# Reordering products and casts in the front stage of a hybrid attention and convolution layer

## The chip, the cores and the metric

The kernel runs on one core of a Trainium2 chip. A core has TensorE (PE, matrix products into PSUM), VectorE (DVE), ScalarE (ACT), GpSimd (POOL) and SyncE (SP), which here issues transfers; each works through its own list of instructions in order, and they meet at semaphores. The metric is the device time of one execution in microseconds, taken as the median of several runs. A profile is one further execution with its own time. PEld is the loading of weights into PE, which overlaps PE's products. "Slab", "chunk" and "half" are words of the kernel, explained below.

## The reference

The layer takes 1024 latent tokens `x` and 256 context tokens `ctx`, each of 1024 numbers, in float32. Cut to what matters:

```python
shift, scale, gate = split(silu(c) @ w_ada + b_ada)          # and the same for c_ctx
h  = rmsnorm(x,   norm_g) * (1 + scale)   + shift
hc = rmsnorm(ctx, norm_g) * (1 + scale_c) + shift_c
q, k, v, za, u, bg, cg, zc = split(h @ w_in)                 # eight groups of 512 columns
kc, vc = split(hc @ w_in[:, 512:1536])
attn = neighbourhood_attention(rms(q), rms(k), v, rms(kc), vc, rpb) * silu(za)
conv = bg * conv3(cg * u) * silu(zc)
out  = x + gate * (concat(attn, conv) @ w_out)
```

The change concerns the first two lines of work: `shift` and `scale` out of `w_ada`, and `h` itself, with the first columns of `h @ w_in`.

## The kernel before

**Numbers in two parts.** Products that need full accuracy are made of three products of rounded parts: a value is split into a high part (a cast, on ACT) and a low part (value minus high part, on DVE), and PE computes high by high, high by low and low by high. So every weight that comes from memory costs a cast on ACT and a subtraction on DVE before PE can use it, and `h` exists as `hh` and `hl`. All instructions issued through the wrapper `ordered` carry line 55 in the profile, so they are told apart by their tiles.

**The front stage** (lines 546 to 880). `w_ada`'s columns for shift and scale come in eight *slabs* of 1024 rows by 256 columns: slab (m, j) gives columns for two of the eight column blocks k = 2m and 2m + 1 of `h`, with j = 0 for shift and 1 for scale. For m = 0 and 1, `products(m, j)` (line 605) multiplies the slab as it is, in plain float32, eight products (16 records in the profile); for m = 2 and 3 `split(m, j, part)` (line 596) first casts the slab in two parts into `slabh` (ACT) and `slabl` (DVE), and `products` then runs 8 products on `slabh` and 8 on `slabl`. The third slabs are those with m = 2, the second ones m = 1. `row_copy(m)` (ACT for m > 0) and `modulation(m)` (four small transposes and a few DVE steps into `ab`) turn the result into per-row shift and scale.

`transposed(half, k)` (line 661) brings column block k of four of x's eight row tiles into PSUM with four PE transposes, and `turn(half, k, on)` (line 667) makes `hh[k]` and `hl[k]` of that half: one ACT activation (`h<-tr`), a second activation or a DVE step (`hw<-tr`, on ACT or DVE by its argument `on`), and a DVE subtraction (`h<-hw,h`). `first_columns(half, k)` (line 686) then runs nine matmuls of 128 by 512 with *chunk* k of `w_in`: three with the high weights (needing `hh`), three with the low weights, three with `hl`.

The tiles of `tr` (line 521) have two buffers. Products of a slab pair hold one from `products(m, 0)` until `modulation(m)` has read it; meanwhile the blocks of transposes share the other, so the next block waits until the `turn` of the one before has read it.

The two functions between which the change moves work on PE (lines 605 to 614 and 661 to 665), shortened:

```python
def products(m, j, kts=range(KT)):
    if m not in mods:
        mods[m] = tr()
    rows = mods[m][:2 if m < 2 else 4, 256 * j:256 * j + 256]
    parts = [(c2, slabs[m, j])] if m < 2 else [(c4, highs[j]), (c4, lows[j])]
    for i, (c, part) in enumerate(parts):
        for kt in kts:
            pe.matmul(rows, c[:, kt], part[:, kt], ...)

def transposed(half, k, ts=range(4)):
    if (half, k) not in pts:
        pts[half, k] = tr()
    for i in ts:
        pe.transpose(pts[half, k][:, i * P:(i + 1) * P], xx[4 * half + i][:, k * P:(k + 1) * P], ident)
```

**Order and transfers.** In this stage the order of the four engines and of SP is the program's order (`strict`, line 524): an instruction waits for the one ahead of it on its engine, however early its own data are there. SP issues all transfers here. Slabs after the first pair share three buffers with `xc` (the context tokens, line 791), with the tables `rw8` (`gains_load`, line 697) and with `rg` (`gains`, line 706): slab (2, 1) goes where (1, 0) was, (3, 0) where (1, 1) was, (3, 1) where (2, 0) was, `xc` where (2, 1) was, the tables where (3, 0) was, `rg` where (3, 1) was. `gains` is four POOL steps that write `rg`; SP stores it to memory (`rope_d<-rg`) and then loads the weights of the projection, `chunk_load(CQ, k)` for k = 0 to 7, into the five buffers `wr`, each of which is free once the cast and the subtraction of an earlier chunk are done (`chunk_split`, line 166: `wh<-wr` on ACT, `wl<-wr,wh` on DVE). Behind these on SP stand `bias_tables` (line 720, 8 and 16 small transfers named `t_d`), and behind them the loads of the next stage.

**After the front stage** the projection runs in 32 tiles `pacc` with products of the convolution's and gates' columns (`pu`) between them, then attention by quarters of heads (scores, exponentials, `po`), and the output projection `pout`. Tiles of the projection are normalised and rotated on ACT and DVE and turned by PE (`trA`, `trB`, line 226). The first unit of gate columns is loaded as `uraw` at the start of that stage (line 1175) and cast on ACT (`uh`).

Of the kernel before, what the change touches and what calls it, by code (L numbers as in the profile page):

```python
# [23 lines left out]
KT = D // P  # L24
# [12 lines left out]
CQ, CK, CV, CZA, CU, CBG, CCG, CZC = (512 * i for i in range(8))  # L37


def body(tc, es, x, ctxt, w_ada, b_ada, w_in, q_g, k_g, rpbr, w_out, vecs, cst, out):  # L40
# [100 lines left out]
    def place(k, shape, dtype, name):  # L141

        return hpool.tile(shape, dtype, name=name, tag=f"h{k}")
# [16 lines left out]
    def chunk_load(col, k):  # L160
        raw = wpp.tile([P, 3, P], F32, name="wr", tag="wr", bufs=5)
        chunk_anchor[:] = [sp.dma_start(raw, bass.AP(w_in.tensor, w_in.offset + (k * P) * 4096 + col,
                                                     [[4096, P], [512, 3], [1, P]]))]
        return raw
# [356 lines left out]
    def tr():  # L521
        return ps0.tile([P, 512], F32, name="tr", tag="tr", bufs=2)
# [9 lines left out]
    def load_slab(m, j):  # L532

        new = place(6 + j, [P, KT, 256], F32, "slab") if m == 0 else sl.tile([P, KT, 256], F32, name="slab", tag="slab", bufs=3)
        n = 2 if m == 0 else 1
        for i in range(n):
            rows = slice(KT // n * i, KT // n * (i + 1))
            sp.dma_start(new[:, rows], bass.AP(w_ada.tensor, w_ada.offset + j * D + 256 * m + 3 * D * P * rows.start,
                                               [[3 * D, P], [3 * D * P, KT // n], [1, 256]]))
        slabs[m, j] = new  # L540

    def load_chunks(ks):
        for k in ks:
            chunks[k] = chunk_load(CU, k)
# [51 lines left out]
    def split(m, j, part):  # L596

        if part == 0:
            highs[j] = hcp.tile([P, KT, 256], F32R, name="slabh", tag="AB"[j])
            lows[j] = place(6 + j, [P, KT, 256], F32R, "slabl")  # L600
        rows = slice(4 * part, 4 * part + 4)
        act.copy(highs[j][:, rows], slabs[m, j][:, rows])
        dve.tensor_tensor(lows[j][:, rows], slabs[m, j][:, rows], highs[j][:, rows].bitcast(F32), ALU.subtract)
# [9 lines that stand above are left out]
                pe.matmul(rows, c[:, kt], part[:, kt], start=(i == 0 and kt == 0 and j == 0),  # L613
                          stop=(i == len(parts) - 1 and kt == KT - 1 and j == 1), skip_group_check=True)
# [25 lines left out]
    def modulated(hi, lo, ps, k, w, on, between=None):  # L640

        n = len(ps.shape) > 2 and 512 or 256
        sh, sc = (ab[:, k, 2 * w + j:2 * w + j + 1] for j in range(2))
        hw = bmp.tile([P, 512], F32, name="hw", tag="kc_s", bufs=2)
        hv = hw[:, :n]
        if n == 512:
            hv = hv.rearrange("p (r b c) -> p r b c", r=8, b=8)
        act.activation(hi, ps, AF.Identity, bias=sh, scale=sc)
        if on is act:
            act.activation(hv, ps, AF.Identity, bias=sh, scale=sc)  # L650
        else:
            dve.tensor_scalar(hv, ps, sc, sh, ALU.mult, ALU.add)
        if between:
            between()
        dve.tensor_tensor(lo, hv, hi.bitcast(F32), ALU.subtract)

    def rows_of(v, half):

        return v.rearrange("p (b r c) -> p r b c", b=8, r=16)[:, 8 * half:8 * half + 8]
# [7 lines that stand above are left out]
    def turn(half, k, on, between=None):  # L667

        modulated(rows_of(hh[k], half), rows_of(hl[k], half),
                  pts.pop((half, k))[:].rearrange("p (r b c) -> p r b c", r=8, b=8), k, 0, on, between)  # L670
# [26 lines left out]
    def gains_load():  # L697

        rw = sl.tile([P, 2048], F32, name="rw8", tag="slab", bufs=3)
        gqk = rw[:, 1024:1152].rearrange("p (n d) -> p n d", n=2)  # L700
        for n, g in enumerate((q_g, k_g)):
            sp.dma_start(gqk[:, n], g.broadcast_to([P, HD]))
        sp.dma_start(rw[:, 0:1024], cst[:, P + 2:P + 1026])
        return rw, gqk

    def gains(tables):

        rw, gqk = tables
        pool.tensor_scalar(gqk[:, 0], gqk[:, 0], 0.125, None, ALU.mult)
        gkc1 = cp.tile([P, 1, HD], F32, name="gkc")  # L710
        pool.tensor_tensor(gkc1[:, 0], gqk[:, 0], gqk[:, 1], ALU.mult)
        rg = sl.tile([P, 2, NB, 2, HD], F32, name="rg", tag="slab", bufs=3)
        for n in range(2):
            rraw = rw[:, 512 * n:512 * n + 512].rearrange("p (b d) -> p b d", d=HD)
            for k in range(2):
                pool.tensor_tensor(rg[:, n, :, k], rraw, gqk[:, k:k + 1].broadcast_to([P, NB, HD]), ALU.mult)
        sp.dma_start(rope_d, rg[:].rearrange("p n b k d -> p (n b k d)"))
        return gkc1[:]
# [52 lines left out]
    turn(1, 0, act)  # L771
    load_slab(2, 1)
    load_chunks([4, 5])
    transposed(1, 1)
    products(1, 1)
    load_slab(3, 0)
    split_chunk(2)
    turn(1, 1, act)
# [7 lines left out]
    modulation(1, rw)  # L786
    turn(0, 2, dve)
    split(2, 0, 1)
    split(2, 1, 0)
    split(2, 1, 1)  # L790
    xc = sl.tile([P, 2, D], F32, name="xc", tag="slab", bufs=3)
    sp.dma_start(xc, ctxt[0].rearrange("(i p) d -> p i d", p=P))
    first_columns(1, 1)
# [2 lines left out]
    for m in range(1, 4):  # L796
        k, new, last = 2 * m, m < 3, m == 3
        turn(1, k, act)
        if m == 2:
            gkc = gains(tables)  # L800
            ch = [chunk_load(CQ, k) for k in range(4)]
        first_columns(0, k)
        transposed(0, k + 1)
        if new:
            products(m + 1, 0)
        turn(0, k + 1, dve)
        if m == 1:
            split(3, 0, 0)
            split(3, 0, 1)
            tables = gains_load()  # L810
        if m == 2:
            for i in range(2):
                square(xc[:, i], i)
            root(0)
            root(1)
            norm(xc[:, 0], 0)
            norm(xc[:, 1], 1)
        if last:
            transposed_ctx(0)
            ch[4] = chunk_split(ch[4])  # L820
            turn_ctx(0)
            bias_tables()
        first_columns(1, k)
        if new:
            split_chunk(k + 2)
            products(m + 1, 1)
            rw = row_copy(m + 1)
        transposed(1, k + 1)
        first_columns(0, k + 1, (0,))
        if last:  # L830
            transposed_ctx(1)
        if new:
            modulation(m + 1, rw)
        turn(1, k + 1, act)
        if new:
            split_chunk(k + 3)
        if m == 1:
            split(3, 1, 0)
        if m == 2:
            ch[0:2] = map(chunk_split, ch[0:2])  # L840
            ch += [chunk_load(CQ, k) for k in (4, 5)]
        if last:
            turn_ctx(1)
        first_columns(0, k + 1, (1, 2))
        if new:
            transposed(0, k + 2)
            if m == 2:
                more_h(range(6, KT))
            turn(0, k + 2, dve)
        if m == 1:  # L850
            split(3, 1, 1)
        if m == 2:
            ch[2:4] = map(chunk_split, ch[2:4])
            ch += [chunk_load(CQ, k) for k in (6, 7)]
        if last:
            group0 = conv_group(0, {u: acc0[n] for n, u in enumerate((CU, CBG, CCG))})
            next(group0)
            do_acts()
            do_dves()
            transposed_ctx(2)  # L860
            ch[5] = chunk_split(ch[5])
            turn_ctx(2)
            first_columns(1, k + 1, (0,))
            transposed_ctx(3)
            ch[6] = chunk_split(ch[6])
            first_columns(1, k + 1, (1,))
            ch[7] = chunk_split(ch[7])
            turn_ctx(3)
            first_columns(1, k + 1, (2,))
        else:  # L870
            first_columns(1, k + 1)
            transposed(1, k + 2)
# [294 lines left out]
    for n in range(NT + 3):  # L1167
# [21 lines left out]
        if t == 0 and 0 < n < NT:  # L1189
            nxt += map(chunk_split, raws)  # L1190
            ch, nxt, raws = nxt, [], []
# [27 lines left out]
        if 1 < n <= NT + 1:  # L1219
            m, r = n - 2, (n - 2) % NB  # L1220
# [218 lines left out]
```

## Time and profile before

| | |
|---|---|
| median of 3 runs | 645.64 us (645.0 to 645.97) |
| profiled execution | 646.57 us, of which the span is 644.8 us |
| granted TensorE clock | 1.0 of full speed |
| PE, busy share of the span | 98% |
| PEld | 83% |
| DVE | 67% |
| ACT | 50% |
| POOL | 20% |

The shares are means over stages with different limits. In a row of the timeline the first number is the start in us from the start of the span, the second how long the group of like instructions lasted; then engine, line, operation, what is written from what, shapes and count, and in brackets the idle time of the engine just before with what ended it. PE's ends are modelled, and consecutive rows of PE overlap by some tenths of a microsecond, so distances are best taken from start to start. "SPq" is SP's queue of transfers: its time is that of issuing, and a merged row of several issues contains the waits between them. A row of the waits gives the waiting engine and tile, what it waited for, the total in us, how often, and the longest.

### The profile page before, as it was taken

To read this page: it belongs to the slowest core of one execution; us is meant where nothing else is said; L and a number is where in the kernel's file an instruction comes from. 1 tells how busy PE (TensorE), PEld (TensorE's weight loads), DVE (VectorE), ACT (ScalarE), POOL (GpSimd) and SP (SyncE) were. 2 spreads that over 40 slices of the span, in tenths; PEclk is the share of its full clock that TensorE was granted. 3 is DMA by queue.
4 is the path that set the end of the run, shared out by engine and by line. 5 is a ranking of instruction groups with operands and counts; after the bars stand their busy time and mean duration, and the time that the engine had idled before them with its cause. 6 is when DMAs were issued, how large, how long until landed. Compare 5 with 4: busy or idle time off the path is not lost.

```text
span 644.8 us, 10300 instructions
## 1 busy us (share of the span) xinstructions
PE 629.4 (98%) x3479; PEld 537.3 (83%) x3480; DVE 432.9 (67%) x819; ACT 322.2 (50%) x692; POOL 130.3 (20%) x138
## 2 busy tenths in 40 slices
PE   8899999999999999999999999999999999999997
PEld 3477798999899999877878888888888888888885
DVE  1677746865775846557787889988998864575111
ACT  3666725533534543438776658565675545352000
POOL 1205003313223231102121111121111111004421
PEclk9999999999999999999999999999999999999999
DMA  8962556778795998799947768886872224976621
GB/s 325 374 227 104 134 186 196 213 219 233 215 278 148 279 267 236 194 236 216 230 114 209 188 149 204 209 211 154 220 166 76 79 79 118 307 236 206 199 98 53
DMA packets 118864, 125.46 MB, mean 195 GB/s; under 512 B 32817, under 2 KB 89353, under 8 KB 117532
## 3 DMA queue, kind: packets, MB, share of 16 engines
q1 hardware_dynamic: 112348, 113.23, 61.7%
q10 hardware_dynamic: 6208, 11.05, 5.8%
q0 software_dynamic: 256, 0.54, 0.3%
q8 instruction: 27, 0.44, 0.3%
q14 instruction: 25, 0.20, 0.1%
HBM read 88.01 MB, written 38.53 MB: 196 GB/s over the span
## 4 chain that ended last, share of the span: by engine, by line
PE 68%; DMA 9%; DVE 8%; ACT 6%; SPq 5%; issue 2%; POOL 2%; ACTq 0%; DVEq 0%; POOLq 0%
PE pu L55 18%; PE pacc L55 17%; PE po L55 5%; PE pout L76 5%; PE pout L75 5%; PE pout L74 4%; DMA v<-v_d 3%; DMA k_s<-k_d 3%; PE tr L55 3%; SPq L55 3%; PE cacc L55 3%; DVE mx L55 2%; PE acc L55 2%; PE pss L55 2%; PE pmx L55 2%
## 5 line engine op out<-in xcount | busy, mean ns | idle before, releaser
L55 PE MATMUL pu<-h,uh 128*128 128x512 f32 x544 | 169.0, 392 | 0.0
L55 PE MATMUL pacc<-wh,h 128*128 128x384 f32 x512 | 135.5, 338 | 0.0
L55 PEld LDWEIGHTS pu<-h,uh 128*128 128x128 f32 x544 | 98.2, 188 | 17.0
L55 PE MATMUL pu<-h,ul 128*128 128x512 f32 x272 | 106.4, 391 | 0.0
L55 PEld LDWEIGHTS pacc<-wh,h 128*128 128x128 f32 x512 | 92.8, 188 | 0.4 <-ACT qn L55 0.4
L55 POOL TENSOR_TENSOR plc<-sc,phc 128x512 fp32r<-128x512 f32 x32 | 42.5, 1330 | 221.1 <-ACT sc L55 99.2
L55 PE MATMUL pacc<-wl,h 128*128 128x384 f32 x256 | 85.6, 334 | 0.0
L55 POOL TENSOR_TENSOR ss<-ss,few 128x4 f32<-128x4 f32 (+1 forms) x40 | 41.9, 1050 | 127.8 <-DVE ss L55 127.4
L55 PEld LDWEIGHTS pu<-h,ul 128*128 128x128 f32 x272 | 51.1, 188 | 11.3
L55 DVE TENSOR_TENSOR mx<-mx,sb 128x384 f32<-128x384 f32 (+1 forms) x64 | 55.6, 877 | 2.0
L75 PE MATMUL pout<-wol,yh 128*128 128x512 f32 x128 | 49.8, 389 | 0.0
L76 PE MATMUL pout<-woh,yl 128*128 128x512 f32 x128 | 49.6, 389 | 0.0
L74 PE MATMUL pout<-woh,yh 128*128 128x512 f32 x128 | 48.3, 389 | 0.0
L55 PEld LDWEIGHTS pacc<-wl,h 128*128 128x128 f32 x256 | 48.1, 188 | 0.1
L55 DVE TENSOR_REDUCE ss<-sq 128x4 f32<-128x260 f32 (+1 forms) x40 | 15.8, 394 | 46.3 <-ACT sq L55 46.3
L55 ACT COPY mg<-pmx 128x256 f32<-128x256 f32 x32 | 12.0, 374 | 58.0 <-PE pmx L55 44.7
L55 ACT ACTIVATE sq<-pacc 128x256 f32<-128x256 f32 x32 | 12.3, 385 | 52.7 <-PE pacc L55 51.8
L1371 DVE TENSOR_TENSOR ot<-pout,gate 128x512 f32<-128x512 f32 x16 | 10.9, 689 | 38.3 <-PE pout L76 36.2
L55 DVE TENSOR_TENSOR pll<-sb,phl 128x768 fp32r<-128x768 f32 (+2 forms) x33 | 29.3, 889 | 7.6 <-ACT sb L55 7.6
L1372 POOL TENSOR_TENSOR ot<-ot,xr 128x512 f32<-128x512 f32 x15 | 20.1, 1351 | 67.9 <-DVE ot L1371 66.5
L55 DVE TENSOR_TENSOR sc<-sc,mg 128x512 f32<-128x512 f32 x32 | 21.8, 683 | 17.5 <-ACT mg L55 17.5
L55 ACT ACTIVATE qn<-pacc,ss 128x64 f32<-128x64 f32 x128 | 30.0, 329 | 6.3 <-POOL ss L55 3.2
(151 smaller groups left out, 1275.9 us busy)
## 6 DMA issues: line engine op xcount, KB each, us to landing
uraw<-in_w_in SPq DMA_DIRECT2D x34, 256.0 KB
q_d<-qs SPq DMA_DIRECT2D x64, 128.0 KB
k_s<-k_d SPq DMA_DIRECT2D x16, 512.0 KB
q_s<-q_d SPq DMA_DIRECT2D x32, 256.0 KB
wr<-in_w_in SPq DMA_DIRECT2D x40, 192.0 KB
slab<-in_w_ada SPq DMA_DIRECT2D x6, 1024.0 KB
t_d<-btw SPq DMA_DIRECT2D x8, 576.0 KB
bt<-t_d SPq DMA_DIRECT2D x8, 576.0 KB
```

The lines of the kernel that those rows point to most:

```text
L55: i = emit(*a, **kw)
L74: i = pe.matmul(ps, ah, bh, start=first, stop=False)
L75: pe.matmul(ps, ah, bl, start=False, stop=False)
L76: pe.matmul(ps, al, bh, start=False, stop=last)
L1371: dve.tensor_tensor(ot, ps, gate[:, cols], ALU.mult)
L1372: (dve if (nh, t) == (1, NB - 1) else pool).tensor_tensor(ot, ot, xr, ALU.add)
```

## The change

Three pieces of program order move; no computation is added or removed, and the buffers stay.

1. `products(1, 1)` is cut after four of its eight row blocks: the first four stand ahead of `transposed(1, 1)`, the other four behind it.
2. The casts of slab (2, 1), `split(2, 1, 0)` and `split(2, 1, 1)`, move from behind `split(2, 0, 1)` to behind `turn(1, 2, act)`, the first statement of the loop's pass m = 1 (k = 2). On PE `first_columns(1, 1)` and `transposed(1, 2)` stand between the two places; SP's load of `xc` is now written ahead of these casts.
3. In the pass m = 2 (k = 4) the casts of the projection's chunks 0 and 1 move from ahead of `turn(0, 6, dve)` to behind it, to those of chunks 2 and 3, and the loads of chunks 4 to 7 are written in the same order as before, chunk 4's ahead of all four casts.

SP's and POOL's lists of instructions are the same before and after, in the same order. The diff, with the statements of the stage around it (a line of "..." stands for statements left out):

```diff
     first_columns(0, 1)
     norm(xx[7], 7)
     products(1, 0)
     transposed(1, 0)
     turn(1, 0, act)
     load_slab(2, 1)
     load_chunks([4, 5])
+    products(1, 1, range(0, 4))
     transposed(1, 1)
-    products(1, 1)
+    products(1, 1, range(4, KT))
     load_slab(3, 0)
     split_chunk(2)
     turn(1, 1, act)
     first_columns(1, 0)
     rw = row_copy(1)
     split_chunk(3)
     split(2, 0, 0)
     load_slab(3, 1)
     load_chunks([6, 7])
     transposed(0, 2)
     modulation(1, rw)
     turn(0, 2, dve)
     split(2, 0, 1)
-    split(2, 1, 0)
-    split(2, 1, 1)
     xc = sl.tile([P, 2, D], F32, name="xc", tag="slab", bufs=3)
     sp.dma_start(xc, ctxt[0].rearrange("(i p) d -> p i d", p=P))
     first_columns(1, 1)
     transposed(1, 2)
 
     for m in range(1, 4):
         k, new, last = 2 * m, m < 3, m == 3
         turn(1, k, act)
+        if m == 1:
+            split(2, 1, 0)
+            split(2, 1, 1)
         if m == 2:
             gkc = gains(tables)
             ch = [chunk_load(CQ, k) for k in range(4)]
         first_columns(0, k)
         transposed(0, k + 1)
         if new:
             products(m + 1, 0)
         turn(0, k + 1, dve)
         if m == 1:
             split(3, 0, 0)
             split(3, 0, 1)
             tables = gains_load()
...
         first_columns(1, k)
         if new:
             split_chunk(k + 2)
             products(m + 1, 1)
             rw = row_copy(m + 1)
         transposed(1, k + 1)
         first_columns(0, k + 1, (0,))
         if last:
             transposed_ctx(1)
         if new:
             modulation(m + 1, rw)
         turn(1, k + 1, act)
         if new:
             split_chunk(k + 3)
         if m == 1:
             split(3, 1, 0)
-        if m == 2:
-            ch[0:2] = map(chunk_split, ch[0:2])
-            ch += [chunk_load(CQ, k) for k in (4, 5)]
         if last:
             turn_ctx(1)
         first_columns(0, k + 1, (1, 2))
         if new:
             transposed(0, k + 2)
             if m == 2:
                 more_h(range(6, KT))
             turn(0, k + 2, dve)
         if m == 1:
             split(3, 1, 1)
         if m == 2:
-            ch[2:4] = map(chunk_split, ch[2:4])
-            ch += [chunk_load(CQ, k) for k in (6, 7)]
+            ch.append(chunk_load(CQ, 4))
+            ch[0:4] = map(chunk_split, ch[0:4])
+            ch += [chunk_load(CQ, k) for k in (5, 6, 7)]
...
         else:
             first_columns(1, k + 1)
             transposed(1, k + 2)
```

In the pass that follows (m = 3, k = 6) the order on PE is `first_columns(0, 6)`, `transposed(0, 7)`, the transposes of `xc` (`transposed_ctx(0)`), `first_columns(1, 6)`.

## The prediction

> **What bounds the kernel now.** I read the page first, for which engine is full; then the waits of TensorE (PE) over the whole span; then the timeline of one engine at a time around the changed lines; last the chain of waits behind them. The page's part 1:
>
> ```profile
> PE 629.4 (98%) x3479; PEld 537.3 (83%) x3480; DVE 432.9 (67%) x819; ACT 322.2 (50%) x692; POOL 130.3 (20%) x138
> ```
>
> PE is busy 98% of the span, so only what shortens PE's own line, or a stall in it, can move the end. Its two longest kinds of stall (engine, waited for, us in total, times, longest):
>
> ```profile
> PE tr L55 <- ACT hw L55: 1.9, 2, 1.5
> PE trA L55 <- DVE rot L55: 1.4, 1, 1.4
> ```
>
> The first lies in the stage that the change touches, the second about 40 us behind it. PE's timeline (start, us, ..., in brackets idle time before and what ended it):
>
> ```profile
> 24.23 3.62 PE L55 MATMUL tr<-slab,c 128*2 128x256 f32 x16
> 27.77 0.65 PE L55 MATMUL tr<-ci,xx 128*128 128x128 f32 x4
> 29.96 0.66 PE L55 MATMUL tr<-ci,xx 128*128 128x128 f32 x4 [1.54 <-ACT hw L55]
> 30.55 3.62 PE L55 MATMUL tr<-slab,c 128*2 128x256 f32 x16
> 34.10 0.96 PE L55 MATMUL acc<-h,wh 128*128 128x512 f32 x3
> ...
> 41.83 0.60 PE L55 MATMUL tr<-ci,xx 128*128 128x128 f32 x4
> 42.84 1.09 PE L55 MATMUL tr<-slabh,c 128*4 128x256 f32 x8 [0.41 <-ACT hw L55]
> ...
> 46.74 1.09 PE L55 MATMUL tr<-slabh,c 128*4 128x256 f32 x8
> ...
> 65.97 0.60 PE L55 MATMUL tr<-ci,xx 128*128 128x128 f32 x4
> 66.32 0.94 PE L55 MATMUL acc<-h,wh 128*128 128x512 f32 x3
> ...
> 68.49 0.60 PE L55 MATMUL tr<-ci,xx 128*128 128x128 f32 x4
> 69.47 0.99 PE L55 MATMUL acc<-h,wh 128*128 128x512 f32 x3 [0.38 <-ACT h L55]
> ...
> 71.84 0.60 PE L55 MATMUL tr<-ci,xx 128*128 128x128 f32 x4
> 72.28 0.60 PE L55 MATMUL tr<-ci,xc 128*128 128x128 f32 x4
> ```
>
> Three stalls stand in it, each ended by ACT. At 29.96 transposed(1, 1) waits until turn(1, 0) has read the one free `tr` buffer. At 42.84 the products of the third slabs wait for turn(1, 2) to do the same. At 69.47 first_columns(0, 6) waits for the first result of turn(0, 6). Because rows of pipelined matmuls overlap, I price by starts: a block of transposes is normally followed 0.35 us later (65.97 to 66.32).
>
> **Part one, products(1, 1) cut in two.** Nothing is added: 16 records take 3.55 us (30.55 to 34.10) whether in one piece or two. After: transposes at 27.77, first half 0.59 later (the distance 29.96 to 30.55) at 28.36, its 8 records to 30.13. The buffer is free at 29.96, so the transposes follow at 30.13 without a wait, the second half at 30.72, first_columns(1, 0) at 30.72 + 1.77 = 32.49 against 34.10: **-1.61**. turn(1, 1) gets its transposes 0.17 later, but its consumer first_columns(1, 1) comes only behind nine matmuls, transposes and modulation, over 3 us on. The half needs slab (1, 1) at 28.36; the view of before shows it used at 30.55 only. Slab (1, 0), issued just ahead on SP, had landed by 24.23, when its products start, and one MB at the some 400 GB/s of this row (DMA, 14 to 27 us, 40 slices) takes 2.6 us:
>
> ```profile
> GB/s 383 413 425 432 416 454 416 416 337 326 403 458 429 441 416 416 403 394 359 381 391 384 378 397 384 378 397 378 384 391 381 388 394 378 373 350 347 348 374 378
> ```
>
> So 26.8 at the latest by this estimate, 1.5 us of cover. Bounds: 0 if the slab came only with its use, -1.8 if the extra switch between products and transposes costs nothing. I take -1.6. SP gains too: slab (3, 0) waits for these products and goes out as much earlier.
>
> **Part two, the third slabs' casts behind turn(1, 2).** ACT and DVE before (the order of every engine and of SP is written out in the code, so nothing else changes place):
>
> ```profile
> 38.51 2.94 ACT L55 CAST slabh<-slab 128x1024 fp32r<-128x1024 f32 x3
> ...
> 67.67 1.07 ACT L55 CAST wh<-wr 128x384 fp32r<-128x384 f32 x2 [2.24 <-DMA wr<-in_w_in]
> 68.64 0.77 ACT L55 ACTIVATE h<-tr,ab 128x512 fp32r<-128x512 f32 x1
> 69.32 0.91 ACT L55 CAST wh<-wr 128x384 fp32r<-128x384 f32 x2
> 70.13 0.78 ACT L55 ACTIVATE h<-tr,ab 128x512 fp32r<-128x512 f32 x1
> 70.81 0.77 ACT L55 ACTIVATE hw<-tr,ab 128x512 f32<-128x512 f32 x1
> ```
>
> ```profile
> 40.10 3.49 DVE L55 TENSOR_TENSOR slabl<-slab,slabh 128x1024 fp32r<-128x1024 f32 x3
> ...
> 70.91 1.02 DVE L55 TENSOR_TENSOR wl<-wr,wh 128x384 fp32r<-128x384 f32 x2
> ```
>
> Of the three casts at 38.51 two (about 1.0 us each) move behind the two activations of turn(1, 2), which last 1.45 (70.13 to 71.58). ACT's work ahead hangs on the second products, so the first cast runs 36.9 to 37.9 after. turn(1, 2) needs its transposes: they start one block of nine matmuls (2.17, 66.32 to 68.49) and 0.35 ahead of 41.83, so after at 37.70, and take 0.60. It runs from 38.4 to 39.85. The products then need no wait: 41.83 - 1.61 + 0.35 = 40.57, against 42.84, together **-2.27**, so part two adds -0.66. The cover is 0.7 us; without it the gain sinks us for us. The moved casts run 39.75 to 41.75 on ACT, their DVE halves (1.16 each) to 43.15, still 0.4 before the old end at 43.59. products(2, 1) wants them at 46.74 - 2.27 = 44.47, 1.3 later. turn(0, 3), one activation of 0.78 on ACT, ends near 42.5. On SP the load of `xc`, into the slab buffer freed at 43.15, and the tables behind it are not late either.
>
> **Part three, the weights' casts behind turn(0, 6).** The four casts go from two ahead and two behind to four behind. Before, ACT sat 2.24 us waiting for chunk 0's transfer with turn(0, 6) queued behind the cast. These transfers are started by SP behind the table store:
>
> ```profile
> 56.03 5.95 POOL L55 TENSOR_TENSOR rg<-rw 128x512 f32<-128x512 f32 x4 [2.48 <-DVE slabl L55]
> ```
>
> ```profile
> 62.38 9.47 SPq L55 DMA_DIRECT2D wr<-in_w_in  x8
> 71.90 1.46 SPq L55 DMA_DIRECT2D t_d<-in_rpb  x2
> ```
>
> POOL's rg starts when DVE's last cast of slab (3, 1) ends (its releaser in the row). ACT and DVE there run on behind products(2, 1), so rg, the store and the loads go forward by 2.27 as PE does. If instead the tables' own load is late, they gain less: its end is not in the view, only that it is no later than 56.03. I take the full shift, since it is queued behind `xc`, which is not late.
>
> After: transposes (0, 6) at 63.70, turn(0, 6) by 65.1, transposes (1, 6) at 66.22, first_columns(0, 6) at 66.57 without a stall. Before it stood 0.63 beyond its normal place (68.49 + 0.35) and lasted 2.37 to the next transposes against 2.17 normally (66.32 to 68.49), since its last third waited for DVE: together **-0.83**, in all -3.10. The price: turn(1, 6) now has four casts ahead of it. Chunks 0 and 1 are there at 65.4 and 65.9 (67.67 and about 68.2, shifted), chunks 2 and 3 at the latest at 67.05 and 67.5 (cast at 69.32 and 69.8). So the casts end between 67.5 and 68.0 and turn(1, 6) between 68.95 and 69.45. The first `xc` transposes need its buffer at 68.74 + 0.44 = 69.18. Bounds of a new stall: 0 and 0.3; I take 0, for the two first chunks came half a us apart and the next two probably did too. DVE's casts for chunk 2 end about 68.2 instead of 71.46, so chunk 7's load and the t_d transfers behind it start about 3.2 earlier.
>
> The Trainium skill (DMA: Bandwidth & Descriptors, Queues, rings and completion order) says that a transfer's completion is signalled only after every earlier write of the same DMA engine. The 2.24 us wait behind the store agrees with it; the rule would tie all four casts to the store, which is the first rival below.
>
> **Beyond the stage.** PE's 1.4 us stall hangs on SP. From the chain of waits:
>
> ```profile
> 92.38 7.09 DMA uraw<-in_w_in
> ...
> 109.80 0.44 PE trA L55 x2
> ```
>
> SP's run of table transfers (from 71.90) ends in this uraw load, ACT's next steps stand behind it, and so do DVE's rotation and PE's trA. PE comes 3.1 earlier, this chain 3.2: the stall stays at 1.3 to 1.4. Everything behind is released by earlier work, so I carry the gain one to one.
>
> **Sum.** -1.61 - 0.66 - 0.83 = -3.10. The profiled execution took 646.57 (span 644.8), 0.93 over the median 645.64; the sum against it is 643.5, against the median **642.5**. Extremes of the terms: -3.3 with all favourable, -2.3 if part three's gain becomes a stall.
>
> **Rivals.**
> First, the chunks' loads move less than PE. If unmoved, chunk 3's cast ends at 70.23 as before, turn(1, 6) at 71.58, and the `xc` transposes start at 71.6 instead of 72.28: -0.7, 644.9, no measurable change. If they move by about 1, 644.0. For it: the tables' landing is not visible. Against: their release comes no later than before.
> Second, SP's chain to uraw stays: PE then only waits longer at 109.80 and the end stays at 645.6. For it: the run of 24 small transfers is limited by SP itself. Against: it starts behind chunk 7's load, which moves.
> Third, slower: the moved third-slab casts delay `xc`, and behind it on SP the tables, rg, the store and the chunks. ACT then holds turn(1, 6) and PE waits at the `xc` transposes. With unmoved chunks 0.7 is left, so beyond 0.7 of delay it is slower than before, us for us; at 2.0 us, 646.9. Against it is the cast end at 43.15, not 43.59.
> The Trainium skill (Perfetto Trace Analysis, Identifying the Most-Contended Engine) says not to judge PE's headroom by matmul busy time but by LDWEIGHTS busy time, 83% here. By that PE is not full and the second rival gains; the waits above, few and short, speak for a full PE, and no run here decides it yet.
>
> **How the numbers follow.** Forecast 0.66 (642.5, own range 641.8 to 643.4). First rival 0.18, of which 0.12 near 644.0 and 0.06 near 644.9. Second 0.08. Third 0.08. Faster by over 0.2% (1.3 us, about what measurement tells): 0.66 + 0.12 = 0.78; same 0.06 + 0.08 = 0.14; slower 0.08. The range takes the forecast and the milder half of the first rival: 641.6 to 644.6.
>
> **What would show it.** Right: no ACT-released stall before the second transposes nor before products(2, 0); first_columns(1, 0) near 32.5; products(2, 0) near 40.6; turn(0, 6) ahead of the chunk casts and no wait of PE for it; `xc` transposes near 69.2; the trA stall still about 1.4 near 106.7. Wrong: a DMA wait of PE at 28.4; ACT waiting for chunk loads later than 67.5; a trA stall grown to 3 or more.

## The result and the profile after

The changed kernel takes **644.25 us** (median, 642.49 to 648.41 in 20 runs) where the kernel before, run beside it, takes 646.16 us (20 runs); the ratio is 0.9967, with a 95% interval of 0.9955 to 0.9979, that is 2.1 us less (1.4 to 2.9). The forecast was 3.1 us less. The miss in the time itself, 644.25 against 642.5, has two parts: the kernel before measured 0.52 higher with 20 runs than with the 3 on which the forecast stood, and the gain is 1.0 to 1.2 us too small (2.1 by the ratio, 1.9 by the two medians). A second measurement of the same two kernels, shown below, gives a ratio of 0.9959, that is 2.6 us less (1.6 to 3.6), an interval that holds the forecast. Pooled, the medians of the two measurements differ by 2.2 us (resampling the runs gives 1.7 to 2.7), which does not hold it.

The profiled execution took 644.16 us. Part 1 of its page, for the kernel after:

```profile
span 642.4 us, 10301 instructions
PE 628.7 (98%) x3479; PEld 537.2 (84%) x3480; DVE 432.3 (67%) x819; ACT 322.1 (50%) x692; POOL 131.6 (20%) x138
```

PE's own work is nearly what it was (629.4 before), so at least 1.7 of the 2.4 us by which the span is shorter are waits that went. PE's waits after, over the whole span (engine, waited for, us in total, times, longest):

```profile
PE pmx L55 <- DVE mx L55: 1.8, 5, 0.7
PE trA L55 <- DVE rot L55: 1.4, 1, 1.4
...
PE acc L55 <- ACT h L55: 0.8, 1, 0.8
PE tr L55 <- DVE ab L55: 0.4, 1, 0.4
```

The row "PE tr <- ACT hw", 1.9 us before, is gone. The wait at trA is as long as it was. PE's timeline after, in the stage of the change:

```profile
28.37 1.89 PE L55 MATMUL tr<-slab,c 128*2 128x256 f32 x8
30.19 0.66 PE L55 MATMUL tr<-ci,xx 128*128 128x128 f32 x4
30.77 1.89 PE L55 MATMUL tr<-slab,c 128*2 128x256 f32 x8
32.59 0.98 PE L55 MATMUL acc<-h,wh 128*128 128x512 f32 x3
...
40.37 0.60 PE L55 MATMUL tr<-ci,xx 128*128 128x128 f32 x4
40.72 1.18 PE L55 MATMUL tr<-slabh,c 128*4 128x256 f32 x8
...
66.45 0.60 PE L55 MATMUL tr<-ci,xx 128*128 128x128 f32 x4
66.81 0.94 PE L55 MATMUL acc<-h,wh 128*128 128x512 f32 x3
...
69.38 0.64 PE L55 MATMUL tr<-ci,xc 128*128 128x128 f32 x4
```

All three stalls have gone: nothing stands in brackets at 30.19, 40.72 and 66.81, and the transposes of `xc` start at 69.38 instead of 72.28, 2.90 earlier (forecast 3.10). So in the stage the change does nearly what it was priced at. What followed is in SP's, ACT's and the chain's rows. SP's queue after:

```profile
60.11 0.33 SPq L55 DMA_DIRECT2D rope_d<-rg  x1
...
67.42 2.30 SPq L55 DMA_DIRECT2D wr<-in_w_in  x3
69.77 0.77 SPq L55 DMA_DIRECT2D t_d<-in_rpb  x1
```

ACT after:

```profile
64.57 0.78 ACT L55 ACTIVATE h<-tr,ab 128x512 fp32r<-128x512 f32 x1 [1.18 <-PE tr L55]
65.73 2.23 ACT L55 CAST wh<-wr 128x384 fp32r<-128x384 f32 x4 [0.39 <-DMA wr<-in_w_in]
67.86 0.78 ACT L55 ACTIVATE h<-tr,ab 128x512 fp32r<-128x512 f32 x1
```

The chain of waits after, at its end for this part:

```profile
90.17 6.22 DMA uraw<-in_w_in
...
106.72 0.44 PE trA L55 x2
```

The bias rows' transfers (`t_d`) start 2.13 us earlier than before (69.77 against 71.90), not 3.2; uraw's second load is issued 2.21 earlier (90.17 against 92.38). That load then took 6.22 us to land instead of 7.09, and only this 0.87 lets trA come 3.08 earlier in this execution (106.72 against 109.80). In executions that give uraw's load the same time before and after, theory A below lets trA come only some 2.2 us earlier. Behind trA this execution loses 0.6 us again: trA comes 3.08 earlier, the span is 2.4 shorter.

### The profile page after: what moved, and what is told of

Its sections match the earlier page's. It is cut to its first block, busy times and chain, and to the rows that moved or that the text cites. A ratio compares the mean times of both kernels' runs of the same rounds, so it can differ in the third digit from the quotient of the medians.

```text
span 642.4 us, 10301 instructions
## 1 busy us (share of the span) xinstructions
PE 628.7 (98%) x3479; PEld 537.2 (84%) x3480; DVE 432.3 (67%) x819; ACT 322.1 (50%) x692; POOL 131.6 (20%) x138
## 4 chain that ended last, share of the span: by engine, by line
PE 66%; DMA 13%; DVE 9%; SPq 6%; ACT 3%; issue 2%; POOL 1%; ACTq 0%; DVEq 0%; POOLq 0%
PE pu L55 18%; PE pacc L55 18%; DMA k_s<-k_d 5%; PE po L55 5%; PE pout L75 4%; PE pout L76 4%; PE pout L74 4%; SPq L55 3%; PE cacc L55 3%; PE acc L55 2%; PE tr L55 2%; DVE mx L55 2%; DVE sb L55 2%; PE pss L55 2%; PE pmx L55 2%
## 5 line engine op out<-in xcount | busy, mean ns | idle before, releaser
L1372 POOL TENSOR_TENSOR ot<-ot,xr 128x512 f32<-128x512 f32 x15 | 20.1, 1345 | 67.5 <-DVE ot L1371 65.9
```

Source lines behind the costliest of these rows:

```text
L1372: (dve if (nh, t) == (1, NB - 1) else pool).tensor_tensor(ot, ot, xr, ALU.add)
```

## The experiments

Two theories were put to the test. **Theory A**: the time behind the first trA is set by uraw's landing, and with it by SP's chain of issues, whose head moved by 2.1 us and not by 3.2; what PE gained beyond that is waited away at trA. **Theory B**: the gain passes trA in full, and a part of it is lost later, in attention and in the output projection.

### Each part alone, and all three again

Each is made from the kernel before, with one part of the diff:

```diff
# p1_products_cut: part one alone
+    products(1, 1, range(0, 4))
     transposed(1, 1)
-    products(1, 1)
+    products(1, 1, range(4, KT))
# p2_slab_casts: part two alone
-    split(2, 1, 0)
-    split(2, 1, 1)
...
         turn(1, k, act)
+        if m == 1:
+            split(2, 1, 0)
+            split(2, 1, 1)
# p3_weight_casts: part three alone
-        if m == 2:
-            ch[0:2] = map(chunk_split, ch[0:2])
-            ch += [chunk_load(CQ, k) for k in (4, 5)]
...
         if m == 2:
-            ch[2:4] = map(chunk_split, ch[2:4])
-            ch += [chunk_load(CQ, k) for k in (6, 7)]
+            ch.append(chunk_load(CQ, 4))
+            ch[0:4] = map(chunk_split, ch[0:4])
+            ch += [chunk_load(CQ, k) for k in (5, 6, 7)]
```

`all_again` is the changed kernel itself.

> Part one alone: products(1, 1) cut in two, the casts as before. By the prediction's sum: first_columns(1, 0) 1.5 to 1.6 us earlier (near 32.5), the stalls before the third slabs' products (0.41) and of first_columns(0, 6) (0.38) still there, all of SP's chain 1.5 earlier, so the trA stall stays near 1.4 and the end is 1.5 us earlier (ratio 0.9977). By the rival that what is gained in front is given back behind: the same stage, but an end less than 1 us earlier.

> Part two alone: the casts of slab (2, 1) behind turn(1, 2). By the prediction's sum: no stall before the third slabs' products, PE and the chain of rg, store and chunk loads 0.6 to 0.7 us earlier, end 0.65 earlier (ratio 0.9990). By the rival: within 0.3 us of the kernel before at the end.

> Part three alone: four chunk casts behind turn(0, 6). By the prediction's sum: first_columns(0, 6) without a stall, the transposes of xc 0.8 us earlier, t_d transfers between 0.5 and 1.4 earlier, end 0.8 earlier (ratio 0.9987). If SP's chain sets what is left behind trA: the end moves only as far as t_d does. If the gain is lost behind: nothing at the end.

> The changed kernel beside its parts on the same chip. Sum of the three parts alone by the prediction: -1.6 - 0.65 - 0.8 = -3.05 us at the xc transposes. Theory A (SP's chain sets what is left behind trA, and it moved by 2.1 only): trA's stall grows where uraw lands as late as before, the end 2 us earlier. Theory B (all of PE's 2.9 to 3.1 us is there behind trA in every execution, and waits for transfers in attention and the output projection take some): trA 3.1 earlier as in the first profile, the loss behind it.

Measured against the kernel before on the same chip (646.48 us):

| kernel | median, us | ratio (95% interval) |
|---|---|---|
| part one alone | 644.71 | 0.9975 (0.9956 to 0.9994) |
| part two alone | 645.84 | 0.9982 (0.9962 to 1.0002) |
| part three alone | 646.93 | 0.9999 (0.9983 to 1.0016) |
| all three | 644.22 | 0.9959 (0.9944 to 0.9975) |

The traces of the four, and those of before and after, by starts in us. "uraw" is the issue of its second load, "landing" the start of ACT's second cast of it, "PE there" the start of the first trA pair, "goes on" that of the second pair, the one that waits:

| kernel | t_d starts | uraw | landing | travel | PE there | goes on | wait |
|---|---|---|---|---|---|---|---|
| before | 71.90 | 92.38 | 99.49 | 7.1 | 107.89 | 109.80 | 1.42 |
| after | 69.77 | 90.17 | 96.41 | 6.2 | 104.80 | 106.72 | 1.43 |
| all three again | 70.29 | 90.03 | 96.10 | 6.1 | 105.19 | 106.40 | 0.72 |
| part one | 71.05 | 91.46 | 98.82 | 7.4 | 107.21 | 109.12 | 1.42 |
| part two | 72.08 | 92.57 | 97.62 | 5.1 | 107.73 | 108.06 | none |
| part three | 71.96 | 91.70 | 99.31 | 7.6 | 107.72 | 109.60 | 1.39 |

Where PE waits there, it goes on 10.29 to 10.31 us after the landing (109.80 - 99.49, 106.72 - 96.41, and so on): uraw's landing sets it, as theory A says. The travel, from issue to landing, differs from execution to execution by 2.5 us, so one execution says little about the shift at trA. The executions also reach the stage at different times: between 17 and 23 us, ahead of every edit, PE's instructions stand later than in before by 0.02 us in after, 0.53 in all three again, 0.49 in part one, 0.60 in part two and 0.35 in part three (medians over like instructions). The starts in a row of the table carry this offset; distances within a row do not.

All three again does not look like theory A. By what was expected of it, A lets the wait grow and B lets trA come 3.1 earlier with a loss behind it. The wait shrank, trA goes on 3.40 earlier (109.80 - 106.40), and the span of 642.7 is only 2.1 shorter, so that 1.3 us were lost behind trA:

```profile
106.40 0.33 PE L55 MATMUL trA<-ci,rot 128*128 128x128 f32 x1 [0.72 <-DVE rot L55]
```

Theory A has the shorter travel to answer with, 6.2 and 6.1 us in the two executions with all three parts against 7.1 in before.

Part three alone shows best what SP's chain does. PE's `xc` transposes start 0.51 earlier than before (71.77 against 72.28), 0.86 with the offset of 0.35 taken off; `t_d` starts 0.06 later, 0.29 earlier with the offset taken off. The time is that of the kernel before with an interval of 1 us to either side, which holds the 0.8 us of the prediction as well as no gain. SP's queue with part three alone:

```profile
62.32 0.33 SPq L55 DMA_DIRECT2D rope_d<-rg  x1
62.70 9.21 SPq L55 DMA_DIRECT2D wr<-in_w_in  x8
71.96 0.77 SPq L55 DMA_DIRECT2D t_d<-in_rpb  x1
```

From the first chunk's load to `t_d` are 9.26 us (71.96 - 62.70), and 9.52 before (71.90 - 62.38, with eight rows of which the last is this one of the kernel before):

```profile
71.48 0.37 SPq L55 DMA_DIRECT2D wr<-in_w_in  x1
```

With the casts together, chunks 5, 6 and 7 are loaded in one burst. In the row of after above the three issues take 2.30 us together, of which the last alone takes 1.30 (68.42 to 69.72) against 0.37 when it stood by itself; with part three alone it takes 1.10 (70.81 to 71.91). So of the 0.9 us by which chunk 7's load was to start earlier beyond the store's shift, SP gave 0.7 to 0.9 back inside that load's issue. Every execution whose 24 small transfers stand in their place shows the like: from the store (`rope_d<-rg`) to the first `t_d` 9.89 to 9.92 us pass in the five without part three (before, part one, part two, and two kernels further down), and 9.64 to 9.77 in the four with it. So part three moves SP's chain by 0.1 to 0.3 us where it moves PE by 0.8. That much is shown; what it does to the time is not.

### Uraw's casts later on ACT

ACT issues uraw's two casts ahead of the projection's scales and so stands at uraw's landing. The edit moves the casts back by two tiles; SP's list is untouched.

```diff
-        if n == 0:
+        if n == 2:
             next(group0)
```

> The kernel before, with ACT's two casts of uraw moved behind the scales of the first projection's tiles, so that ACT no longer stands at uraw's landing while TensorE needs ACT's output at the first trA. Theory A (uraw's landing, which follows SP's chain of issues, sets the time behind trA): the 1.42 us that PE waits at the first trA go, the stage behind it starts about 1.4 us earlier, and the time is about 1.4 us below that of the kernel before (645.1 beside 646.5). Theory B (the landing costs nothing that the later stages do not give back anyway): the wait may go, the time stays within 0.5 us of the kernel before.

> The changed kernel with the same move of uraw's two casts. Theory A: no wait at the first trA, whose start then follows the TensorE stream alone and stands 2.9 to 3.0 us ahead of the same kernel without the three parts; the time is 2.9 below that of the kernel before with the same move, and about 1.4 below the changed kernel. Theory B (part of the gain is lost behind trA, in attention and in the output projection): trA moves by 2.9 to 3.0 as well, but the time is only about 2 us below the kernel before with the same move.

Measured: the kernel before with this move 646.11 us, ratio to the kernel before 1.0001 (0.9979 to 1.0022); the changed kernel with it 643.11 us, ratio 0.9944 (0.9924 to 0.9964). The wait is gone in both; PE's timeline of the changed kernel with the move:

```profile
105.30 0.27 PE L55 MATMUL trA<-ci,rot 128*128 128x128 f32 x1
105.41 0.27 PE L55 MATMUL trA<-ci,qn 128*128 128x128 f32 x1
105.63 0.27 PE L55 MATMUL trA<-ci,rot 128*128 128x128 f32 x1
```

No bracket stands at the second pair, and it comes 0.33 behind the first, where with the wait it came 1.9 behind. So the wait hung on ACT standing at uraw, not on the work of the rotation itself. The two differ by 3.0 us in their medians (646.11 - 643.11), where theory A expects 2.9 and B 2; but their runs scatter, and resampling both sets puts the difference between 0.6 and 5.1. The first of the two misses its own expectation by its ratio: without the wait, it should have been 1.4 us below the kernel before, and the ratio says no gain, with an interval of 1.4 us to either side. Its median is 1.3 below the 647.41 of the kernel before on the same chip, but resampling gives from 2.4 below to 0.8 above, for three of its twelve runs took more than 648. Its profiled execution has a span of 643.4 us, 1.4 below that of the kernel before, but one execution is no median. So the pair shows where the wait comes from, and its times decide nothing. The changed kernel's gain by the move, 0.9944 beside 0.9967 and 0.9959, goes the way of theory A, but the intervals overlap. The move has a price, too: in the changed kernel PE now stops 0.36 us ahead of the first gate products (`pu`, at 110.67), where it did not stop without the move.

### Parts one and two without part three

```diff
# against the changed kernel
+        if m == 2:
+            ch[0:2] = map(chunk_split, ch[0:2])
+            ch += [chunk_load(CQ, k) for k in (4, 5)]
...
         if m == 2:
-            ch.append(chunk_load(CQ, 4))
-            ch[0:4] = map(chunk_split, ch[0:4])
-            ch += [chunk_load(CQ, k) for k in (5, 6, 7)]
+            ch[2:4] = map(chunk_split, ch[2:4])
+            ch += [chunk_load(CQ, k) for k in (6, 7)]
```

> The changed kernel without its third part: the projections' casts and loads stand where they stood before. Theory A: the last load is issued alone again (0.37 us instead of 1.30), the transfers of the bias rows and uraw's load start as early as with all three parts, and the time is that of the changed kernel within 0.4 us. Theory B: the third part is worth its 0.83 us of TensorE time at the end too, so this run is about 0.8 us above the changed kernel.

Measured: 644.87 us, ratio 0.9962 (0.9946 to 0.9978), beside 0.9967 and 0.9959 for the changed kernel. The ratios lie together, as theory A has it, but their intervals are wide enough for theory B's 0.8 us as well. The medians differ by 0.6 (644.87 against 644.25 and 644.22; resampling gives -0.3 to 1.1), between the two theories. In the trace the last load is alone again (0.37), and from the store to `t_d` 9.89 us pass (70.66 - 60.77) against 9.66 and 9.67 in the two executions with all parts; uraw's second load is issued at 90.42, 0.25 and 0.39 behind them. So here too the third part moves SP's chain by 0.2 to 0.4 us, not by 0.8; the time doesn't settle it.

### Eight transfers of the bias rows early

The chain itself can be shortened. Of the 24 small transfers, the first 8 read only an input; SP has nothing to issue between the tables' load near 48 and the store near 60. The edit puts the 8 there and leaves the 16 where they were.

```diff
     def bias_tables():
         for kc in range(8):
             sp.dma_start(t2_d[kc], ...)
+
+    def bias_rows():
         t2 = t2_d[:]
         for kr in range(16):
             sp.dma_start(t3_d[:, kr], ...)
...
             tables = gains_load()
+            bias_tables()
...
             turn_ctx(0)
-            bias_tables()
+            bias_rows()
```

> The changed kernel with 8 of the 24 small transfers of the bias rows issued earlier, behind the load of the gains, where SP has nothing to issue. Theory A: the 16 that stay end some 7 us earlier, uraw's load is issued about as much earlier, its landing is no longer the last thing ahead of the first trA, the wait of 1.4 us there goes, and the time is about 1.4 us below the changed kernel (some 642.8). Theory B: the wait goes, the time stays within 0.5 us of the changed kernel.

> The kernel before, with the same 8 transfers of the bias rows issued early. Theory A: uraw lands well ahead of its need, the wait of 1.42 us at the first trA goes, and the time is about 1.4 us below the kernel before. Theory B: no change beyond 0.5 us.

> The changed kernel without its third part, with the 8 transfers issued early. Theory A: with uraw out of the way TensorE's own stream sets the first trA, so the third part now counts: this run starts trA about 0.8 us later than the changed kernel with the 8 transfers early, and takes about 0.8 us more. Theory B: the third part is worth nothing anyway, so the two are within 0.3 us in time.

> The changed kernel with the 8 transfers early, as before, beside its two companions on one chip. Theory A: 3.1 us below the kernel before with the same transfers early, and 4.5 below the kernel before. Theory B: 2.1 below its companion, for part of the gain is lost behind trA whether uraw is late or not.

| kernel, with the 8 transfers early | median, us | ratio to the kernel before (95% interval) |
|---|---|---|
| changed | 642.39 | 0.9927 (0.9906 to 0.9948) |
| before | 645.03 | 0.9977 (0.9964 to 0.9991) |
| changed, without part three | 642.85 | 0.9940 (0.9923 to 0.9957) |
| changed, again | 642.26 | 0.9932 (0.9913 to 0.9952) |

The kernel before took 647.01 us beside the last three and 647.41 beside the first. SP's queue of the changed kernel with the early transfers (the second run of it):

```profile
66.83 1.98 SPq L55 DMA_DIRECT2D wr<-in_w_in  x3
68.86 10.95 SPq L55 DMA_DIRECT2D t_d<-t_d  x16
79.92 0.38 SPq L55 DMA_DIRECT2D rope<-rope_d  x1
86.14 0.26 SPq L55 DMA_DIRECT2D gacc<-in_b_ada  x1
86.50 0.93 SPq L55 DMA_DIRECT2D uraw<-in_w_in  x2
```

The 16 end at 79.8, over 8 us earlier than the changed kernel's (77.31 + 10.91 = 88.2). But uraw is not issued 7 us earlier, as the expectation had it: the load of `gacc` (a row for the layer's output gate) stands ahead of it on SP and now waits for POOL to clear `gacc`. The waits of SP in the first run of this kernel, between 60 and 100 us:

```profile
SPq L55 <- POOL gacc L55: 5.6, 1, 5.6
```

So uraw's first load is issued only 2.7 us earlier (86.50 here, 89.18 after). It also lands sooner once issued. The instructions of tile uraw in the second run of this kernel:

```profile
L55 SPq DMA_DIRECT2D uraw<-in_w_in x2: 384/438/492, 86.5 to 86.9; - x2
L55 ACT CAST uh<-uraw x2: 621/622/622, 90.7 to 91.3; 128x512 fp32r<-128x512 f32 x2
```

and of the kernel before with the early transfers:

```profile
L55 SPq DMA_DIRECT2D uraw<-in_w_in x2: 384/438/492, 90.2 to 90.6; - x2
L55 ACT CAST uh<-uraw x2: 620/620/620, 94.0 to 94.6; 128x512 fp32r<-128x512 f32 x2
```

The last start in each row is that of the second issue and of the second cast: 4.4 and 3.9 us of travel where the six kernels of the table above had 5.1 to 7.6. Both effects together bring the landing forward by 5 us, and in none of these kernels does PE wait at trA; in the changed one the second pair comes at 104.42, with no bracket:

```profile
104.20 0.27 PE L55 MATMUL trA<-ci,qn 128*128 128x128 f32 x1
104.42 0.27 PE L55 MATMUL trA<-ci,rot 128*128 128x128 f32 x1
```

What follows. On the kernel before, the 1.42 us wait gone is worth 1.5 us (0.9977; 0.6 to 2.3), as theory A says; B had 0.5 at most, just outside. (The move of uraw's casts took the same wait away and showed nothing, with an interval that overlaps this one.) It bears on what the prediction left open: a stall of PE taken out comes back as time, as it does with part one alone (a wait of 1.54 gone, 1.6 us less), so PE's line sets the end although weight loads fill only 83% of it. The Trainium skill (Perfetto Trace Analysis, Identifying the Most-Contended Engine) names that share, with the share of peak FLOP/s, as the measure of how close PE is to its peak; no run here tests that, and the prediction's step from it to the second rival does not follow. With uraw out of the way the three parts together are worth 2.8 us (645.03 - 642.26; resampling both sets of runs gives 2.3 to 3.5), against 2.2 in the same way without the early transfers (pooled from both measurements of the changed kernel; 1.7 to 2.7). The forecast of 3.1 lies inside the first interval and outside the second, and theory B's 2.1 just outside the first; but the two intervals overlap (their difference, resampled, is -0.1 to 1.5), so that uraw took some 0.6 us of the gain is likely and not shown. Part three is worth 0.6 us in the medians (642.85 - 642.26; resampling gives -0.6 to 1.6) and one microsecond at trA (105.42 against 104.42 for the second pair); A expected 0.8 of both, B under 0.3 in time. With 6 runs of one of them the time alone doesn't decide.

### Both moves

The changed kernel with the 8 transfers early and with uraw's casts later.

> The changed kernel with both moves: 8 transfers of the bias rows early, and ACT's casts of uraw behind the first scales. Theory A: each of the two moves alone takes the wait at the first trA away, so both together give no more than one: the time of the changed kernel with the transfers early, within 0.4 us. Theory B has no number of its own here; a gain beyond 0.5 us would say that ACT's casts cost something besides that wait.

Measured: 642.71 us, ratio 0.9952 (0.9925 to 0.9978), beside 642.26 and 0.9932 for the early transfers alone on the same chip. The second move adds nothing that the runs show once the first has taken the wait away, as theory A says. The best version is the changed kernel with the 8 transfers early: 0.9932 (0.9913 to 0.9952), measured twice; its medians lie 2 us below the changed kernel's (resampling gives 1.3 to 2.6).

### What is left for theory B

The traces were laid over each other, start by start of like PE instructions, each against the one execution of the kernel before. Between 300 and 360 us (attention) the shift grew worse by 0.25 us in after, by 1.3 in all three again, by 0.8 in part one and in part three, and by nothing in part two. The early-transfer kernels show the same spread with both signs: 0.8 lost in one execution of the changed kernel, 1.6 in the other, and 0.8 gained without part three. The same kernel differs from itself there by about 1 us. Part of it shows in PE's waits on DVE's running maximum (the pmx row above): 1.3 us in before; 1.8 in after, 2.1, 2.1 and 2.4 in three other executions with all three parts; but 1.1 and 1.3 in those two with uraw's casts later, 2.4 in part three alone, and 1.6 in part two, which lost nothing there. So a single execution gains or loses up to some 1.5 us in attention.

Over all that follows, from the second trA pair to the end of the span, the fourteen executions took 534.5 to 536.9 us: 535.0 in before, 535.6 in after and 536.3 in all three again, on average 535.7 in the six with all three parts and 535.4 in the eight others. That is 0.3 more where single executions scatter by 0.7 (one standard deviation), so a loss of the missing microsecond there is neither shown nor excluded. Theory A is no further: the wait at trA that it expects to grow by some 0.4 to 0.9 us was 1.43 and 0.72 in the two executions of the changed kernel and 1.42 in before. For A speak the issue times and the 2.8 us with uraw out of the way; for B both executions of the changed kernel as it stands.

## Why the prediction was right or wrong

**Part one** was right: second transposes at 30.19 (forecast 30.13), first_columns(1, 0) at 32.59 (32.49), a gain of 1.51 for 1.61, and no DMA wait at 28.37. Alone it is worth 0.0025 of the time, 1.6 us (0.4 to 2.8).

**Part two** was right: products(2, 0) at 40.72 without a wait (forecast 40.57), 2.12 earlier for 2.27; products(2, 1) at 44.70 were not held up by the later casts. Alone 1.2 us (from 2.5 of gain to 0.1 of loss), which its own runs do not tell from nothing.

**Part three** was right on PE, ACT and the chunks' order: turn(0, 6) at 64.57 ahead of the casts, first_columns(0, 6) at 66.81 without a stall (66.57), the four casts 65.73 to 67.96, turn(1, 6) at 67.86 (range 67.5 to 68.0), `xc` transposes at 69.38 (69.18). The store and the loads moved by 1.90 and not 2.27 (rope_d<-rg from 62.01 to 60.11), since PE and so slab (3, 1)'s casts moved by 2.1 and rg, waiting for them, by 1.94:

```profile
54.09 5.99 POOL L55 TENSOR_TENSOR rg<-rw 128x512 f32<-128x512 f32 x4 [1.16 <-DVE slabl L55]
```

**The step that failed** stands at the end of part three's working: "chunk 7's load and the t_d transfers behind it start about 3.2 earlier". Chunk 7's load did start 3.06 earlier (68.42 against 71.48). The transfers behind it started 2.13 earlier, for the load, now third of a burst, took 1.30 us to issue instead of 0.37. The prediction read the load's *start* from DVE's cast and gave its issue the old length. Uraw's load inherits the 2.1 (2.21), and the sentence "PE comes 3.1 earlier, this chain 3.2" became PE 3.09 (104.80 against 107.89) and chain 2.2. With that, "the stall stays at 1.3 to 1.4" came true by luck: it was 1.43 in the first execution of the changed kernel because uraw's load travelled 0.87 us less, and 0.72 in the second.

That this lag of SP's chain is the microsecond missing in the time is argued, not shown. For it, uraw's issue moved by 2.2 us and the time by 2.1, and the two pairs without the wait differ by 2.8 and 3.0 us, with intervals that do not exclude the other reading. Against it, in both executions of the changed kernel trA goes on 3.1 and 3.4 us earlier and the spans are only 2.4 and 2.1 shorter: in these it is "Everything behind is released by earlier work, so I carry the gain one to one" that fails, behind trA. Executions scatter by as much, so the cause of the missing microsecond stays open.

**The rivals.** The second, that SP's chain to uraw stays, came nearest: the chain moved by two thirds of what PE did, and not by nothing. But the longer wait at trA that it foresaw is in neither execution. The first was mostly refuted: the chunks' loads moved by 1.9 us, more than the one microsecond that it was priced at, although its 644.0 happens to be near the time, by luck. The third did not occur: `xc`, the tables and rg were all earlier. Of the sentence on the Trainium skill (DMA: Bandwidth & Descriptors, Queues, rings and completion order), the store's tie to the casts was not tried by itself; ACT's wait for chunk 0 fell from 2.24 to 0.39 only because turn(0, 6) was put ahead of it.

## What to carry to other kernels

When PE is full, a reordering that takes its stalls away must be followed to the next place where PE meets a transfer; there the queue's issue times, each with its own length, say how far the transfer moves. A cast brought forward releases loads earlier but also closer together, and in six of seven executions here one load of such a burst took 0.98 to 1.41 us to issue instead of 0.37; price the start of the *next* issue, not of this one. If such a queue has transfers without any dependence, put them into its idle time first: here that was worth about as much again as the change itself (2.0 us beside 2.2). And one pair of traces does not tell where a microsecond went: executions of the same kernel differ by as much in a single stage.

## What the hardware showed that was not expected

- A load's issue on SP's queue took 0.37 us alone. With part three, three loads are issued within 1.0 to 1.6 us. In five executions the third of them took 1.06 to 1.41 us, in one the second took 0.98, and in one (both moves) none took over 0.43; there the small transfer behind them took 1.09, against 0.68 to 0.69 in the four others with the early transfers.
- From the issue of uraw's second load to the cast that needs it 5.1 to 7.6 us passed when small transfers had been issued until some 2 us ahead of it, and 3.6 to 4.4 when SP had stood still for some 6 us but for `gacc`'s load. These are different executions of like kernels, so the cause, the earlier transfers' traffic, is argued and not shown.
- DVE's subtraction of 128 by 512 (h<-hw,h), 0.69 us elsewhere, took 1.64 in after when it started within the first step of POOL's rg (from 54.09). DVE after, ahead of rg and within it:

```profile
52.05 0.69 DVE L55 TENSOR_TENSOR h<-hw,h 128x512 fp32r<-128x512 f32 x1
...
54.28 1.64 DVE L55 TENSOR_TENSOR h<-hw,h 128x512 fp32r<-128x512 f32 x1 [0.28 <-ACT hw L55]
...
56.98 0.69 DVE L55 TENSOR_TENSOR h<-hw,h 128x512 fp32r<-128x512 f32 x1
```

That agrees with the Trainium skill (SBUF — State Buffer, Who interferes with whom), by which a DVE instruction with two inputs in SBUF contends with a POOL instruction that reads SBUF. The third row stands within rg as well and took 0.69; it started 0.05 us ahead of rg's third step (57.03), and there the POOL step was the longer one, 1.80 against 1.30 in the kernel before (58.98). It cost PE nothing here, since PE has no wait between 50 and 62 us.
